# Three loads of one seam moved from SyncE's queue to ScalarE's, in a hybrid mixer block on one Trainium2 core

## The chip, the cores and the metric

The kernel runs on 1 core of one Trainium2 chip. The metric is the device time of one execution in microseconds (us), the median over runs. A core has five engines with queues of their own: TensorE (PE, matmuls; PEld is its weight load), VectorE (DVE), ScalarE (ACT), GpSimd (POOL) and SyncE (SP). In this kernel SP issues nearly all transfers, ACT issues some stores, and each queue runs its instructions strictly in order: what stands behind a waiting instruction waits too.

## The reference

One encoder layer in float32, with 512 frames of width 2048: an input projection, two recurrent mixers (a gated delta rule and RWKV-7), an output projection, cross-attention into 256 memory tokens, and a squared-ReLU MLP.

```python
y = rmsnorm(x) @ W_in
h = x + concat[gdn(y_gdn), rwkv7(y_rwkv)] @ W_out
mn = rmsnorm(mem)                      # 256 memory tokens
k = mn @ wk;  v = mn @ wv              # keys and values
h = h + softmax((rmsnorm(h) @ wq) k^T / sqrt(512)) v @ wo      # 4 heads
h = h + relu(rmsnorm(h) @ w_up)**2 @ w_down
out = rmsnorm(h)
```

## The kernel before, in words

Every float32 weight is split into a rounded part `whi` and a rest `wlo`, and the activations likewise (`xhi`, `xlo`), so a product of near float32 precision takes three fast matmuls. For each weight tile of 128x1024 (512 KB) SP loads `wraw`, ACT casts it to `whi`, DVE subtracts to get `wlo`, and PE multiplies. Three buffers of each kind take turns (`NWR`, `NWS` = 3): the load of tile i+3 can only go out when DVE has finished with tile i.

The first phase, about 0 to 1126 us of the span, is laid out by a planner in the kernel itself. Its functions are generators, called chains, which yield single instructions: `loader` (the weight tiles), `projections` (the matmuls), `rwkv` and `gdn` (the mixers), `presums` and others. `run` keeps a clock per engine, estimates with `cost` when each chain's next instruction could start, and writes the one that could start first, with a chain's rank as a handicap. What comes out is a fixed order per engine. Since every choice follows from the estimates, one different choice early on can shift the whole order behind it. A transfer enters the estimates in `issue`: it costs its queue's clock 330 ns on SP and 60 ns on ACT, and it is taken to land 2.9 us after its issue or later, if earlier transfers fill the bandwidth.

The list `wq` holds the sources of all tiles in their order. Tiles 0 to 117 are the input projection (59 groups `py`, 2 tiles each), with four passes of the memory tokens between them for their squares. Then comes the seam that this document is about, entries 122 to 127: three quarters of the memory tokens (`in_memT`), the first key weight tile (`in_wk`), the last quarter of the memory tokens, the second key weight tile. 30 more key tiles follow and then 32 of the query weights (`in_wqT`). The function `rawload(i)` takes a buffer and yields the load of entry i; `loader` calls it for entry i+3 when it is done with entry i. The function `memory` turns a quarter of the memory tokens into four tiles `mhl` (ACT scales, DVE takes the rest). PE goes from the last `py` over to `kp` (keys, 16 groups of two weight tiles) and then to `kq` (the query weights times the keys). Each `kp` half needs `whi` and `wlo` of one key tile and 8 of the 16 `mhl`.

Between these matmuls the mixers' work is woven in. Here it is: the norm of a GDN key (`gn` on PE, `sg` on ACT, then `gkn`, `gk` on DVE, then `pkk` on PE); and the triangular inverse of the last RWKV pair, whose small blocks POOL solves in `sr`, whose results go out by SP as `bg16T` and `bg16U`, come back as `r` and `E`, and are multiplied together by PE in `ri7x`, `ri7w`, `ri7s`, `ri7t` and `ri7u`, with `k` and `r` updated by DVE in between. The later `gi7` and `gs` are the same for the last GDN head.

`presums` works ahead for the MLP: it loads four blocks of `w_down` in pieces of 410 columns (`ds`), adds and subtracts them on DVE and stores the sums in DRAM. It runs at the lowest priority until the keys are done; what is left over is done in pieces of up to 512 columns (`sl`, `acc`) in the MLP's second half, between 2369 and 2652 us.

Of the kernel before, what the change touches and what calls it, by code (L numbers as in the profile page):

```python
# [73 lines left out]
def build(tc, I, out):  # L74
    nc = tc.nc
# [64 lines left out]
    def wraw():  # L140
        wcnt[0] += 1
        return tile_of(pw, [P, 1024], F32, "wraw", f"wraw{wcnt[0]}", NWR)
# [32 lines left out]
    def tile_of(pool, shape, dt, tag, nm, bufs):  # L175
        t = pool.tile(shape, dt, tag=tag, name=nm, bufs=bufs)
        turns[tag] = turns.get(tag, -1) + 1
        slot[t.tensor.name] = (tag, turns[tag] % bufs)
        holder[tag, turns[tag] % bufs] = t.tensor.name
        return t  # L180
# [27 lines left out]
    DV, AC, GS, TE, SY = (Lane(e, k) for e, k in ((V, "DVE"), (S, "ACT"), (GP, "POOL"), (PE, "PE"), (nc.sync, "SP")))  # L208
# [169 lines left out]
    wq = [("w", I["w_in"][n][:, h * 1024:(h + 1) * 1024]) for h in range(2) for n in range(2)]  # L378
# [36 lines left out]
    wq += [("m", m) for m in mem4[:3]] + hk[:1] + [("m", mem4[3])] + hk[1:]  # L415
    wq += [("w", I["wqT"][n][:, g * 1024:(g + 1) * 1024]) for n in range(KD) for g in range(2)]
    NKP, NKQ = 2 * NIN, 2 * NIN + 2 * KD
    raws, halves, used, whole, piece = {}, {}, set(), set(), {}

    def pieceload(i):  # L420
        piece[i] = tl("sg", 512, NSH["sg"])
        return SY.dma_start(piece[i], wq[i][1][:, 0:512])

    def rawload(i):
        raws[i] = wraw()
        if i in piece:
            return SY.dma_start(raws[i][:, 512:], wq[i][1][:, 512:])
        o = raws[i] if len(wq[i][1].shape) == 2 else raws[i].rearrange("p (a b) -> p a b", b=M)
        return SY.dma_start(o, wq[i][1])

    def loader():
        w = nm = 0
        for i, (kind, _) in enumerate(wq):
            yield lambda: i in raws
            if kind == "w":
                if w in (2, 3):
                    hi, lo = (tile_of(pm, [P, 1024], F32R, t, f"w{t}", 1) for t in ("BK", "AR", "GA", "GB")[2 * w - 4:2 * w - 2])
                else:
                    prev = (w if w < 2 else w - 2) - NWS
                    if prev >= 0:  # L440
                        yield lambda: prev + 2 * (prev > 1) in used
                    hi, lo = halves[w] if w in piece else wsplit()
                if w in piece:
                    yield after("piece", w)
                    yield from split_(raws[i][:, 512:], hi[:, 512:], lo[:, 512:])
                else:
                    yield from split_(raws[i], hi, lo)
                    halves[w] = hi, lo
                whole.add(w)
                w += 1  # L450
            else:
                yield from (memory if kind == "m" else squares)(nm % 4, raws[i])
                nm += 1
            if NWR < i + NWR <= 2 * NWR:
                chain(late(i + NWR), 2)
            elif i + NWR < len(wq):
                yield rawload(i + NWR)
# [7 lines left out]
    def late(i):  # L465
        yield lambda: len(xr) == KD and i - 1 in raws
        yield rawload(i)
# [793 lines left out]
    issue(pieceload(1))  # L1261
    issue(xload(1))
    issue(rawload(0))
    issue(rawload(1))
    for k in range(2, 6):
# [1153 lines left out]
```

## Time and profile before

| | before |
|---|---|
| median of 3 runs | 2902.2 us (2902.17 to 2905.29) |
| profiled execution, its own time | 2904.46 us |
| its span (first to last instruction) | 2902.7 us |
| PE busy | 2870.4 us (99%) |
| DVE, ACT, POOL busy | 2330.4, 1570.0, 223.6 us |
| mean granted TensorE clock | 0.998 |
| seam (last `py`, first `kp`) | about 900 to 938 us of the span |

The span is what the profile covers; 1.8 us of the execution's own time lie outside it. A row of the trace's timeline gives start and length in us, the engine, the line (L256 is the planner's `issue`-time helper, so nearly every planned instruction carries it), the operation, what it writes and reads, and in brackets the idle time ahead of it with what ended that. SPq and ACTq are the transfers' issues on the two queues; their length is the issue, not the transfer. A view of windows gives for each stretch its length, the busy time of PE, PEld, DVE, ACT and POOL with their instruction counts, the granted clock of TensorE (1.00 is full speed), the busy share of the DMA engines and GB/s.

### The profile page before, as it was taken

What the parts mean: (1) busy time and instruction counts of PE and PEld (TensorE: products, weight loads), DVE (VectorE), ACT (ScalarE), POOL (GpSimd) and SP (SyncE); (2) the same over time, 40 slices, a digit from 0 to 9 for tenths busy, and PEclk for the clock granted to TensorE, in tenths of its full rate; (3) what the DMA queues carried; (4) which work ended last, traced back from release to release, by engine and by line L of the source; (5) the groups of instructions that cost most, each with busy time, mean ns of one, the idle gap of its engine ahead of it and who ended that gap; (6) DMA issues with size and microseconds to landing.
All of it is one profiled execution on the core that took longest, in us unless ns stands there. A gap on an engine that the chain in (4) does not pass through costs nothing.

```text
span 2902.7 us, 49242 instructions
## 1 busy us (share of the span) xinstructions
PE 2870.4 (99%) x18794; PEld 2420.3 (83%) x18794; DVE 2330.4 (80%) x3547; ACT 1570.0 (54%) x2233; POOL 223.6 (8%) x547
## 2 busy tenths in 40 slices
PE   8999999999999999999999999999999999999998
PEld 7877877787877888889988888888888888888887
DVE  7787787787887877769956898898998878787888
ACT  6454555555655655564445656555555645454544
POOL 0213213213223000000000000000000000000000
PEclk9999999999999999999999999999999999999999
DMA  5646656656666788784423354565566868978733
GB/s 190 175 139 184 164 156 181 160 150 187 176 163 188 219 249 280 227 286 159 127 92 95 106 163 152 193 199 193 186 201 191 283 225 278 295 257 272 270 100 109
DMA packets 319773, 553.02 MB, mean 191 GB/s; under 512 B 100968, under 2 KB 186220, under 8 KB 319536
## 3 DMA queue, kind: packets, MB, share of 16 engines
q1 hardware_dynamic: 292144, 518.41, 58.0%
q10 hardware_dynamic: 27392, 31.46, 3.1%
q8 instruction: 147, 2.41, 0.3%
q14 instruction: 90, 0.74, 0.1%
HBM read 443.45 MB, written 106.31 MB: 189 GB/s over the span
## 4 chain that ended last, share of the span: by engine, by line
PE 93%; DMA 3%; DVE 2%; ACT 1%; issue 1%; POOL 0%; ACTq 0%; SPq 0%; DVEq 0%; POOLq 0%
PE py L256 22%; PE mxu L256 12%; PE mgu L256 6%; PE mgd L256 6%; PE mxd L256 6%; PE op L122 6%; PE vp L122 3%; PE sc L122 3%; PE at L122 3%; PE mmd L256 3%; PE kp L256 3%; PE mmu L256 3%; PE scrd L256 3%; PE scgd L256 3%; PE kq L256 3%; PE vo L122 1%
## 5 line engine op out<-in xcount | busy, mean ns | idle before, releaser
L256 ACT CAST whi<-wraw 128x1024 fp32r<-128x1024 f32 (+1 forms) x366 | 383.7, 1049 | 399.8 <-PE py L256 146.8
L256 DVE TENSOR_TENSOR wlo<-wraw,whi 128x1024 fp32r<-128x1024 f32 (+1 forms) x366 | 450.4, 1231 | 102.7 <-ACT whi L256 92.9
L256 PE MATMUL py<-xhi,whi 128*128 128x512 f32 x928 | 372.2, 401 | 7.8 <-ACT xhi L256 7.8
L256 PE MATMUL py<-xlo,whi 128*128 128x512 f32 x928 | 373.7, 403 | 0.0
L256 PE MATMUL py<-xhi,wlo 128*128 128x512 f32 x928 | 372.9, 402 | 0.0
L256 ACT CAST whi<-w 128x1024 fp32r<-128x1024 f32 x176 | 185.4, 1054 | 203.9 <-PE mxu L256 48.3
L256 DVE TENSOR_TENSOR wlo<-w,whi 128x1024 fp32r<-128x1024 f32 x176 | 214.8, 1221 | 51.5 <-ACT whi L256 49.5
L256 PE MATMUL mxu<-cb,whi 128*128 128x512 f32 x1016 | 255.0, 392 | 0.0
L256 PEld LDWEIGHTS py<-xhi,whi 128*128 128x128 f32 x928 | 175.0, 189 | 42.1 <-ACT xhi L256 7.8
L256 PEld LDWEIGHTS mxu<-cb,whi 128*128 128x128 f32 x1016 | 182.8, 189 | 32.7
L256 PEld LDWEIGHTS py<-xlo,whi 128*128 128x128 f32 x928 | 175.0, 189 | 35.5 <-DVE xlo L256 0.9
L256 PEld LDWEIGHTS py<-xhi,wlo 128*128 128x128 f32 x928 | 175.1, 189 | 35.1 <-issue 1.8
L131 DVE TENSOR_TENSOR wlo<-wraw,whi 128x1024 fp32r<-128x1024 f32 x112 | 136.6, 1221 | 45.5 <-ACT whi L130 42.5
L130 ACT CAST whi<-wraw 128x1024 fp32r<-128x1024 f32 x112 | 117.7, 1051 | 85.5 <-PE op L122 29.1
L256 PEld LDWEIGHTS mxu<-cb,wlo 128*128 128x128 f32 x1016 | 138.7, 190 | 10.5 <-DVE wlo L256 0.7
L256 PE MATMUL mxu<-cb,wlo 128*128 128x256 f32 x1016 | 142.2, 282 | 0.3 <-DVE wlo L256 0.3
L256 ACT ACT_TABLE_LOAD x87 | 111.6, 1283 | 36.4 <-DVE suml_gn L256 15.5
L256 PE MATMUL mgu<-cb,whi 128*128 128x512 f32 x512 | 129.4, 394 | 1.4 <-ACT whi L256 1.3
L256 PE MATMUL mxd<-whi,cb 128*128 128x512 f32 x512 | 126.7, 389 | 0.0
L256 PE MATMUL mgd<-whi,cb 128*128 128x512 f32 x512 | 126.5, 389 | 0.0
L256 ACT CAST whi<-ws 128x1024 fp32r<-128x1024 f32 x75 | 78.9, 1052 | 75.4 <-PE mgu L256 49.2
L122 PE MATMUL op<-ob,whi 128*128 128x256 f32 (+1 forms) x752 | 115.3, 304 | 0.0
(946 smaller groups left out, 6452.3 us busy)
## 6 DMA issues: line engine op xcount, KB each, us to landing
wraw<-in_w_in SPq DMA_DIRECT2D x116, 512.0 KB, 4.5
wraw<-in_w_up SPq DMA_DIRECT2D x65, 512.0 KB, 3.8
w<-in_w_up SPq DMA_DIRECT2D x63, 512.0 KB, 3.9
ds<-in_w_dm SPq DMA_DIRECT2D x128, 205.0 KB, 4.0
sd_s<-ds SPq DMA_DIRECT2D x128, 205.0 KB, 5.2
wraw<-sd_s SPq DMA_DIRECT2D x51, 512.0 KB, 5.1
w<-sd_s SPq DMA_DIRECT2D x50, 512.0 KB, 5.0
w<-in_w_dm SPq DMA_DIRECT2D x48, 512.0 KB, 5.1
```

Source lines behind the costliest of these rows:

```text
L122: PE.matmul(o, l, r, start=start, stop=stop, skip_group_check=again)
L130: S.copy(hi, src)
L131: V.tensor_tensor(out=lo, in0=src, in1=hi.bitcast(F32), op=ALU.subtract)
L256: f(*a, **k)
```

## The change

Entries 125, 126 and 127 of `wq` (the first key tile, the last quarter of the memory tokens, the second key tile) are issued by ACT instead of SP. `QM` is the entry of the first memory quarter of the seam, 122. Nothing else is edited, and the three transfers are the same as before.

```diff
+    SY_ = SY
     raws, halves, used, whole, piece = {}, {}, set(), set(), {}
 
     def pieceload(i):
         piece[i] = tl("sg", 512, NSH["sg"])
         return SY.dma_start(piece[i], wq[i][1][:, 0:512])
 
+    QM = next(i for i, q in enumerate(wq) if q[0] == "m")
+
     def rawload(i):
         raws[i] = wraw()
+        SY = Lane(nc.scalar, "ACT") if i - QM in (3,4,5,) else SY_
         if i in piece:
             return SY.dma_start(raws[i][:, 512:], wq[i][1][:, 512:])
```

Since the planner prices the three loads differently, it lays out anew what follows, up to about the sixth step of `kq`. From there to the MLP the order on PE, DVE, ACT and SP is as before. Of the summing ahead, 39 pieces of 410 columns instead of 40 are done in the first phase, and the MLP's second half has one piece of `sl` and `acc` more.

On ACT, at the seam (`sg` is the norm of the GDN key, `mhl` the memory tokens), a piece of the difference:

```order
 L256 ACTIVATE sg_10407<-gk_10186 128x512
+L256 DMA wraw_10409<-in_wk 128x1024
+L256 ACTIVATE mhl_10418<-wraw_10149,prm 128x256
+L256 ACTIVATE mhl_10424<-wraw_10149,prm 128x256
+L256 ACTIVATE mhl_10430<-wraw_10149,prm 128x256
+L256 ACTIVATE mhl_10435<-wraw_10149,prm 128x256
 L256 CAST sumh_gn_0_10411_10412<-sg_10407 128x512
```

The first key tile's load stands right behind the first quarter of `mhl` and the square `sg`; the second quarter of `mhl` now precedes the cast for the norm.

Further on in the same queue, of the changed kernel alone (`wraw_10440` is the last memory quarter, `whi_10490` the first key tile's cast):

```order
L256 DMA wraw_10473<-in_wk 128x1024
L256 CAST whi_10490<-wraw_10409 128x1024
L256 ACT_TABLE_LOAD
L256 ACTIVATE sg_10407<-sg_10407 128x512
L256 COPY rstd<-y_184 128x256
L256 ACTIVATE mhl_10519<-wraw_10440,prm 128x256
```

Before, both halves of the norm (`sg`) and their table loads stood ahead of the third quarter of `mhl`, and the key tile's cast came after all of that.

On SP, in the same place, a piece of the difference (`bg16U`, `r`, `E` are the RWKV inverse on its way through DRAM, `sd` the sums' stores):

```order
 L256 DMA bg16U<-sr_10130 64x16x16
-L256 DMA wraw_10409<-in_wk 128x1024
 L256 DMA r_10390<-bg16T 64x8x64 x2
 L256 DMA E_565_10391<-bg16U 64x4x64 x4
-L256 DMA wraw_10446<-in_memT 128x1024
 L256 DMA sd_1_s_154<-ds_55_829 128x410
-L256 DMA wraw_10498<-in_wk 128x1024
```

The three loads leave the places behind the inverse's transfers; the third key tile's load is the first one left on SP, behind three stores of sums.

On DVE, where the RWKV inverse's `k` is made for PE, first before and then in the change:

```order
L256 SCALAR_TENSOR_TENSOR mhl_10528<-wraw_10446,prm,mhl_10528 128x256
L256 TENSOR_TENSOR gEs_10331<-pkk_10504,gEs_10331 128x512
L256 TENSOR_TENSOR wlo_10541<-wraw_10498,whi_10540 128x1024
L256 TENSOR_TENSOR k_10468<-ri7x_10469,cst 128x256
L256 TENSOR_TENSOR k_10468<-ri7w_10470,cst 128x256
L256 TENSOR_TENSOR wlo_10581<-wraw_10508,whi_10580 128x1024
```

```order
L256 SCALAR_TENSOR_TENSOR mhl_10542<-wraw_10440,prm,mhl_10542 128x256
L256 TENSOR_TENSOR wlo_10548<-wraw_10473,whi_10547 128x1024
L256 TENSOR_TENSOR wlo_10575<-wraw_10505,whi_10574 128x1024
L256 TENSOR_TENSOR k_10479<-ri7x_10480,cst 128x256
L256 TENSOR_TENSOR k_10479<-ri7w_10481,cst 128x256
L256 TENSOR_TENSOR gEs_10331<-pkk_10530,gEs_10331 128x512
```

The first `k` stood behind the rest of the second key tile; now it stands behind the rest of the third one too (`wlo_10575`).

On PE, where the last GDN head goes from its inverse (`gi7u`) to its recurrence (`gs`), of the change alone:

```order
L256 MATMUL kp_11748<-mhl_10542,wlo_11713 128x256
L256 MATMUL gi7u_11723<-TtG,gkn_11687 64x64 x4
L256 MATMUL gs_7_0_11832<-gv_11489,TtG 128x128
L256 MATMUL kq_0_0_11834<-khl_10666,whi_11750 128x512
L256 MATMUL kq_0_0_11834<-khl_10717,whi_11750 128x512
```

Before, ten `kp` matmuls stood between `gi7u` and the first `gs`, which reads the `TtG` that DVE makes of `gi7u`; now none does.

## The prediction

> **What bounds the kernel now.** I read the page's head and its chain first, then the windows by stage, the waits of PE, and last the timelines of all queues at the seam.
>
> ```profile
> PE 2870.4 (99%) x18794; PEld 2420.3 (83%) x18794; DVE 2330.4 (80%) x3547; ACT 1570.0 (54%) x2233; POOL 223.6 (8%) x547
> PE 93%; DMA 3%; DVE 2%; ACT 1%; issue 1%; POOL 0%; ACTq 0%; SPq 0%; DVEq 0%; POOLq 0%
> ...
> 900.00:920.00 20.00, 16.58 (x108) 13.41 (x106) 11.37 (x23) 13.01 (x24) 7.79 (x21) 1.00 0.74 189
> 920.00:940.00 20.00, 16.74 (x272) 13.68 (x273) 14.09 (x24) 9.48 (x16) 7.69 (x19) 0.91 0.60 178
> 960.00:980.00 20.00, 20.00 (x180) 17.90 (x179) 18.61 (x36) 9.85 (x16) 0.00 (x0) 1.00 0.63 180
> ...
> PE kp L256 <- ACT whi L256: 2.4, 1, 2.4
> PE pkk L256 <- DVE gk L256: 2.2, 1, 2.2
> PE ri7u L256 <- DVE k L256: 2.0, 1, 2.0
> ```
>
> PE sets the time: it is busy 99% and makes up 93% of the chain. A change can only gain where PE idles or runs slowly, and of 32.3 us of idle time in the whole span (2902.7 less 2870.4) 6.7 lie in the two windows of the seam. The three wait rows are those gaps: 2.2 + 2.4 + 2.0 = 6.6 us. A second loss shows in the clock column, which falls below 1.00 in the second window; in slices of 2 us:
>
> ```profile
> 930.00:932.00 2.00, 0.04 (x1) 0.00 (x0) 1.59 (x3) 1.70 (x3) 1.02 (x2) 1.00 0.26 99
> 932.00:934.00 2.00, 1.97 (x65) 1.71 (x66) 1.97 (x5) 0.21 (x2) 1.61 (x6) 0.84 0.58 145
> 934.00:936.00 2.00, 2.00 (x6) 1.56 (x5) 2.00 (x4) 1.20 (x4) 1.76 (x4) 0.50 0.40 135
> 936.00:938.00 2.00, 2.00 (x12) 1.71 (x11) 0.63 (x1) 0.84 (x1) 1.69 (x5) 0.80 0.75 240
> ```
>
> Behind the third gap the clock is 0.84, 0.50 and 0.80 for 2 us each: 2 x (0.16 + 0.50 + 0.20) = 1.7 us of full-speed work lost. What the seam could give at most is 6.6 + 1.7 = 8.3 us, 0.29% of the time.
>
> Now the cause of the gaps, from the timelines and the chain of waits:
>
> ```profile
> 903.81 0.29 POOL sr L256
> 906.87 0.63 POOL sr L256
> ...
> 906.84 0.58 SPq L256 DMA_DIRECT2D bg16T<-sr  x1
> 908.23 4.19 DMA wraw<-in_wk
> 914.51 5.56 DMA wraw<-in_wk
> 922.46 6.77 DMA wraw<-in_wk
> ...
> 901.47 1.78 DVE L256 SCALAR_TENSOR_TENSOR mhl<-wraw,prm,mhl 128x256 fp32r<-128x256 f32 x4 [0.31 <-ACT mhl L256]
> 911.84 0.69 DVE L256 TENSOR_TENSOR y<-py,rstd 128x512 f32<-128x512 f32 x1 [0.95 <-PE py L256]
> 918.25 1.71 ACT L256 ACTIVATE mhl<-wraw,prm 128x256 fp32r<-128x256 f32 x4 [4.33 <-DMA wraw<-in_memT]
> 920.10 1.04 ACT L256 CAST whi<-wraw 128x1024 fp32r<-128x1024 f32 x1
> 929.33 1.05 ACT L256 CAST whi<-wraw 128x1024 fp32r<-128x1024 f32 x1 [3.60 <-DMA wraw<-in_wk]
> ```
>
> The first key tile's buffer is free when DVE is done with the first memory quarter, at 901.47 + 1.78 = 903.25. SP issues its load only at 908.23, because `bg16T` stands ahead of it and waits until about 906.8 for POOL's solve. The last memory quarter and the second key tile queue up behind that. ACT stands 4.33 us at 918.25 for the memory quarter; the second key tile is cast only at 920.10, and PE's second gap ends there. The third gap has the same root, a tile that landed late, and `k` behind its rest on DVE.
>
> **The change, step by step.** I walk the new orders with the old durations, to see what remains of each gap.
>
> ```profile
> 902.54 0.62 ACT L256 ACTIVATE sg<-gk 128x512 f32<-128x512 f32 x1
> 905.44 1.28 ACT L256 ACT_TABLE_LOAD   x1
> 906.73 0.69 ACT L256 ACTIVATE sg<-gn,cb_e 128x512 f32<-128x512 f32 x1
> 913.95 1.23 DVE L256 TENSOR_TENSOR wlo<-wraw,whi 128x1024 fp32r<-128x1024 f32 x1
> 913.98 1.16 PE L256 MATMUL pkk<-gk,gkn 128*128 128x128 f32 x8 [2.18 <-DVE gk L256]
> 921.20 1.87 PE L256 MATMUL kp<-mhl,whi 128*128 128x512 f32 x7 [2.44 <-ACT whi L256]
> 932.03 0.33 PE L256 MATMUL ri7u<-E,k 64*64 64x64 f32 x4 [1.98 <-DVE k L256]
> 933.46 3.63 PE L256 MATMUL kp<-mhl,whi 128*128 128x512 f32 x8
> ...
> ud<-sl ACTq DMA_DIRECT2D x48, 256.0 KB, 3.9
> xd<-ab ACTq DMA_DIRECT2D x8, 512.0 KB, 3.7
> L256 ACTq DMA_DIRECT2D ud<-sl x48: 364/367/422, 1664.5 to 2282.5; - x48
> ```
>
> *ACT.* Three issues at 0.37 us (the ACTq row) are 1.1 us more on ACT. The first load goes out at 903.3, since `sg` ends at 903.2 and DVE is done at 903.25; ACT hardly waits. The second memory quarter (1.7) and the norm's cast (0.6) take ACT to 905.9; DVE is done with that quarter at about 906.1, so the memory load goes out at 906.2. The third quarter follows until 908.2, a table load until 909.5, the norm's logarithm until 910.1; the second key load goes out at 910.1 to 910.5. The first key tile's cast is 910.5 to 911.5, the second table load and exponential end at 913.4, a copy at 913.7, the last memory quarter at 915.4. How long a load lands on ACT's queue at this place no row shows. The trace bounds it by the key loads on SP, 4.2 and 6.8 us; the stores of ACT's queue lie lower (3.7, 3.9). I take the middle row, 5.6, because it stands in the same crowded stretch. At any of them the first load and the memory quarter are there before ACT comes to them (903.6 + 6.8 = 910.4; 906.5 + 6.8 = 913.3).
>
> *First gap.* PE ends `py` at about 911.8, the cast is done at 911.5, so `kp` starts at once. `pkk` has been moved behind it: the exponential ends at 913.4, then `gkn` and `gk` on DVE (of the size of `y`, 0.69 each) give about 915.0, while PE is through with the first tile at 914.7. Remaining: 0.3 of 2.2.
>
> *Second gap.* The second key tile lands at 910.5 + 5.6 = 916.1, its cast is done at 917.1; PE needs it after `pkk`, at about 916.0. Remaining: 1.1 of 2.4 (0 with a landing of 4.2, 2.3 with 6.8).
>
> *A new wait.* `ri7s` needs `k`, which DVE now does behind the rest of the third key tile. That load stays on SP and goes out when the first tile's rest is done, at 911.84 + 0.69 + 1.23 = 913.8; it lands at 919.4, its cast ends at 920.4, its rest at 921.7, and `k` at 922.4. PE has run out of other work at about 920.3. New: 2.1 us (0.7 to 3.4 with the two bounds).
>
> *Third gap.* The second `ri7u` needs a `k` behind the rest of the sixth key tile. Tile six goes out when tile three's buffer is free (921.7), lands at 927.3, is cast and split by 929.8, and with `khl` and the two `k` steps it is 931.5 to 932.4. PE gets there, with the 15.0 us of work that lies between in the trace (911.8 to the `kp` row at 933.46, less 6.6), one and a half key tiles of 3 us more, and the waits so far, at about 933. Remaining: 0 of 2.0.
>
> Sum at the seam: 6.6 - (0.3 + 1.1 + 2.1) = 3.1 us gained, between 0.9 and 5.6 with the bounds of the landing. The slow clock: it fell after three gaps of at least 2.0 us within 20 us. With one such gap left I take it to stay at 1.00, a gain of 1.7, and keep 0 as the other end.
>
> The Trainium skill's page "TensorE: Matmul & The Clock Gate", Part 1: The HAM clock gate, has the clock halved after an idle window of about 3.4 us and given back after a busy one; the windows run freely. The trace agrees on the half clock and on some 4 us until it is back, but no idle stretch here is longer than 2.44 us, so the condition as the page puts it isn't met and the measurement decides. By its window an estimate of one fall is 3.4 x 0.5 = 1.7 us, the same size.
>
> *Behind the seam.* PE is then earlier by 4.8 us and fully busy, so the lead carries to the end unless something is late. One place is, the last GDN head:
>
> ```profile
> 1025.09 0.38 PE L256 MATMUL gs<-gv,TtG 128*128 128x128 f32 x2
> 1025.51 0.29 DVE L256 COPY gE<-gs 128x128 f32<-128x128 f32 x1 [1.34 <-PE gs L256]
> 1025.90 0.44 PE L256 MATMUL gs<-gE,gkt 128*128 128x128 f32 x2
> 1032.32 0.64 PE L256 MATMUL kq<-khl,whi 128*128 128x512 f32 x2
> ...
> 2620.00:2660.00 40.00, 40.00 (x178) 33.10 (x177) 27.62 (x31) 15.03 (x16) 0.00 (x0) 1.00 0.92 310
> 2660.00:2700.00 40.00, 40.00 (x178) 33.14 (x177) 33.24 (x41) 22.45 (x28) 0.00 (x0) 1.00 0.66 219
> ```
>
> From one `gs` through DVE's copy to the next takes 0.8 us. With no matmul between `gi7u` and the first `gs`, PE waits that trip: 0.8 lost (0 to 2, if a weight tile's rest of 1.2 comes in between on DVE). The next steps have three `kp`-sized matmuls between them, which about cover it.
>
> *The summing ahead.* One piece less in the keys takes four subtractions of 410 columns off DVE. One more piece in the MLP is 8 transfers of 256 KB, 2.1 MB or 6.8 us at 310 GB/s. It comes after 2652 us, beside the window at 2660 with a DMA share of 0.66, and PE made its 178 matmuls per 40 us unslowed even beside the pieces at 0.92. I cost it at nothing; without that cover it is up to 6.8.
>
> Sum: -3.1 - 1.7 + 0.8 = -4.0 us. The profiled execution took 2904.5 us (span 2902.7 and 1.8 around it), which would become 2900.5. The median of the runs, 2902.2, is 2.3 lower, so I forecast 2902.2 - 4.0 = 2898.2 us.
>
> **The rivals.**
> *All three waits go.* If the loads land in 4.2 us, the third key tile too, and the order absorbs the rest, the whole 8.3 less 0.8 comes off: 2902.2 - 7.5 = 2894.7. For it: DMA share is 0.74 at the seam, and the loads now start earlier. Against: `k` stands behind the third tile.
> *The loads move, the time doesn't.* DVE is at 18.61 of 20 us around 970. If PE arrives earlier and DVE can't, PE waits there and the lead is given back: 2902. For it: that row. Against: DVE idled in the seam (11.37 of 20 at 900), so it can also start earlier. The Trainium skill's page "DMA: Bandwidth & Descriptors", section Issuing engines are not separate DMA queues, says that transfers from SP and ACT share the same 16 DMA engines and that a second issuing engine saves only issue time; by that rule this rival is right. The row at 908.23, 5 us behind a free buffer, speaks against it here: what the load loses is not bandwidth but its place behind a waiting instruction.
> *Slower.* The new order between 920 and 1031 has more places like the first `k`, where a step of an inverse or recurrence stands on DVE behind the rest of a tile still on its way. Each costs what the third gap did, 2.0. From two such places on the gain is gone; five of them and one more fall of the clock make -4.0 + 10.0 + 1.7 = +7.7, 2909.9. For it: the third gap was just that, in an order made by the same estimates (2.9 us for a landing that took 4.2 to 6.8). Against: in the window at 960, of the same stage, PE idled nowhere (20.00 of 20).
>
> **How the numbers follow.** Chances: forecast 0.46, all waits gone 0.20, no change 0.16, slower 0.18. About 0.2% (5.8 us, from 2896.4 to 2908.0) is what a measurement of this kernel can tell from no change. Of the forecast a third lies below 2896.4, of the second case nine tenths: faster 0.34. Of the slower case two thirds are past 2908.0: slower 0.12. Within: 0.54. Range: from 2894, all waits gone, to 2906.5, short of the slower case's end; the forecast's own is 2895.5 to 2901.5.
>
> **What would show it.** In the changed profile the first key load is an ACTq row near 903.5 and PE's first `kp` follows `py` with no gap; ACT's 4.33 us for the memory quarter is gone; `ri7s` waits about 2 us for `k` near 921; the clock is 1.00 from 930 to 940; the first `kq` starts about 4 us before 1032.3, and that lead stays in every later stage. I am wrong if a wait of PE for `k`, `gs` or `whi` between 930 and 1040 adds up to more than 4 us, or the lead shrinks between 2650 and 2740.

## The result, and the profile after

The changed kernel takes 2910.9 us (median of 7 runs, 2909.5 to 2912.8); the kernel before, on the same chip, 2902.2 us. The ratio is 1.0033 with a 95% interval of 1.0024 to 1.0042. It is 8.7 us slower, past the bound of 0.2%. I had forecast 2898.2 us, with 12% for slower: the sign was wrong.

From the page of the changed kernel, its windows of 20 us and its list of PE's waits (columns as before: busy time of PE, PEld, DVE, ACT and POOL, then the granted clock):

```profile
PE 2873.7 (99%) x18794; PEld 2423.1 (83%) x18794; DVE 2333.6 (80%) x3547; ACT 1570.9 (54%) x2233; POOL 223.5 (8%) x547
...
900.00:920.00 20.00, 15.90 (x63) 12.83 (x62) 13.69 (x24) 13.59 (x25) 7.67 (x20) 0.85 0.73 185
920.00:940.00 20.00, 18.48 (x277) 15.37 (x279) 14.66 (x25) 9.55 (x15) 3.18 (x8) 0.97 0.75 209
...
PE kp L256 <- ACT whi L256: 7.4, 2, 4.1
PE gs L256 <- DVE TtG L256: 2.0, 1, 2.0
PE ri7s L256 <- DVE k L256: 1.5, 1, 1.5
```

PE still sets the time. Two of the three gaps of before are gone as waits (`pkk` for `gk`, `ri7u` for `k`); the wait of `kp` for `whi` has grown from 2.4 to 7.4 us in two pieces, and `gs` for `TtG` and `ri7s` for `k` are new. The first piece, 4.1 us, lies in the seam. The second, 3.3 us, and the 2.0 us of `gs` lie behind 980, where PE of the kernel before idled 0.3 us. Three stages of PE, first of before, then of the changed kernel, show the whole (busy time, clock, DMA share, GB/s):

```profile
905.00:985.00 80.00, 73.31 (x680) 0.98 0.67 193
985.00:1030.00 45.00, 44.70 (x337) 1.00 0.78 243
1030.00:1080.00 50.00, 50.00 (x298) 1.00 0.81 247
```

```profile
905.00:985.00 80.00, 74.38 (x685) 0.96 0.66 187
985.00:1030.00 45.00, 41.72 (x295) 0.96 0.68 214
1030.00:1080.00 50.00, 48.00 (x290) 0.97 0.68 205
```

What PE loses in a stage is its idle time plus its busy time times what the clock lacks to 1.00. In the seam (905 to 985) that is 6.7 + 1.5 = 8.2 us before and 5.6 + 3.0 = 8.6 after: nothing gained. Behind it, before lost 0.3 us; after loses 3.3 + 1.7 from 985 to 1030 and 2.0 + 1.4 from 1030 to 1080, 8.4 in all. (The clock column has two digits, so each clock term is good to 0.4 us.) The difference of 8.5 us comes near the 8.7 us of the medians, but that closeness is in part chance: the two profiled executions differ by only 5.9 us in span (2908.6 and 2902.7), and outside these stages the one of before idles 1.3 us more. From the end of the last `py` to the end of `kq` the changed kernel takes 7.7 us longer (221.7 against 214.0). So the stages show where the time goes, and its sum to some 3 us. In this account moving the loads costs nothing on balance where they were moved, and the time goes where the planner laid the order anew.

**In the seam**, the timelines of ACT, SP and PE of the changed kernel, and its clock in a slice of 2 us:

```profile
903.37 0.39 ACTq L256 DMA_DIRECT2D wraw<-in_wk  x1
906.13 0.34 ACTq L256 DMA_DIRECT2D wraw<-in_memT  x1
909.59 0.69 ACT L256 ACTIVATE sg<-gn,cb_e 128x512 f32<-128x512 f32 x1
914.12 0.35 ACTq L256 DMA_DIRECT2D wraw<-in_wk  x1
914.51 1.04 ACT L256 CAST whi<-wraw 128x1024 fp32r<-128x1024 f32 x1 [4.23 <-DMA r<-bg16T]
...
906.20 0.58 SPq L256 DMA_DIRECT2D bg16T<-sr  x1
911.18 1.27 SPq L256 DMA_DIRECT2D r<-bg16T  x2
...
915.61 3.78 PE L256 MATMUL kp<-mhl,whi 128*128 128x512 f32 x8 [4.10 <-ACT whi L256]
...
916.00:918.00 2.00, 2.00 (x6) 0.50 0.98 225
```

The first key tile and the memory quarter go out where I put them, at 903.4 and 906.1. The second key tile does not: ACT is free at 910.3 and issues it at 914.1. The releaser named is a transfer of the other queue, the first `r<-bg16T`, issued at 911.18. The first key tile has landed by then (the packets of both earlier loads on ACT's queue are over by 910), but it is cast behind that issue; PE stands for it 4.1 us and then runs at half clock. `bg16T` itself is late: from its issue to that of `r`, which waits for its landing, it is 4.98 us, where before it was 2.53 (906.84 to 909.37).

**Behind 980** two things wait, in the timelines of SP, ACT and PE, and of DVE and PE:

```profile
985.53 1.41 SPq L256 DMA_DIRECT2D sd_s<-ds  x3
991.06 1.28 SPq L256 DMA_DIRECT2D ds<-in_w_dm  x3
992.44 0.38 SPq L256 DMA_DIRECT2D wraw<-in_wk  x1
998.63 1.04 ACT L256 CAST whi<-wraw 128x1024 fp32r<-128x1024 f32 x1 [5.53 <-DMA wraw<-in_wk]
999.73 3.59 PE L256 MATMUL kp<-mhl,whi 128*128 128x512 f32 x8 [3.28 <-ACT whi L256]
...
1033.52 0.68 PE L256 MATMUL gi7u<-TtG,gkn 64*64 64x64 f32 x8
1033.79 1.23 DVE L256 TENSOR_TENSOR wlo<-wraw,whi 128x1024 fp32r<-128x1024 f32 x1 [0.40 <-ACT whi L256]
1034.93 0.42 DVE L256 TENSOR_TENSOR y<-kp,rstd 128x256 f32<-128x256 f32 x1
...
1035.72 0.41 DVE L256 COPY TtG<-gi7u 64x256 f32<-64x256 f32 x1
1036.19 0.49 PE L256 MATMUL gs<-gv,TtG 128*128 128x128 f32 x2 [2.00 <-DVE TtG L256]
```

At 985.5 SP issues three stores of sums; the loads behind them refill the buffers that those stores read, so SP stands until the first store has landed, at 991.06, 5.5 us after its issue. The planner lands a store 2.9 us after its issue, and so put a key tile behind those loads. It goes out at 992.4, lands 6.1 us later, and PE waits 3.3 us. Near 1034 the copy to `TtG` stands on DVE behind the rest of a weight tile and two steps of `y`.

### The profile page after: what moved, and what is told of

It reads as the page before. It is cut to its first block, busy times and chain, and to the rows that moved or that the text cites. A ratio compares the mean times of both kernels' runs of the same rounds, so it can differ in the third digit from the quotient of the medians.

```text
span 2908.6 us, 49252 instructions
## 1 busy us (share of the span) xinstructions
PE 2873.7 (99%) x18794; PEld 2423.1 (83%) x18794; DVE 2333.6 (80%) x3547; ACT 1570.9 (54%) x2233; POOL 223.5 (8%) x547
## 4 chain that ended last, share of the span: by engine, by line
PE 92%; DMA 3%; DVE 2%; ACT 2%; issue 1%; POOL 0%; SPq 0%; ACTq 0%; POOLq 0%; DVEq 0%
PE py L256 21%; PE mxu L256 12%; PE mgu L256 6%; PE mxd L256 6%; PE mgd L256 6%; PE op L122 5%; PE vp L122 3%; PE mmu L256 3%; PE sc L122 3%; PE at L122 3%; PE scrd L256 3%; PE scgd L256 3%; PE mmd L256 3%; PE kq L256 3%; PE kp L256 2%; PE vo L122 2%
```

## The experiments

Each run is compared with runs of the kernel before on its own chip; medians of two chips are not compared. In several kernels single instructions are issued later than planned, with the planner's clocks untouched, by these lines in `issue` (numbers count the calls of `issue`):

```diff
+        LOG[0] += 1
+        n = LOG[0]
+        if n in HOLD:
+            held.setdefault(HOLD[n], []).append((f, a, k))
+        else:
+            f(*a, **k)
+            for f_, a_, k_ in held.pop(n, []):
+                f_(*a_, **k_)
-        f(*a, **k)
```

### What holds ACT: a completion semaphore

In the built program every transfer signals one of eight completion semaphores, given out in turn, and its issue waits for the transfer that had the semaphore last. Both rows of the changed program name number 5, with seven transfers between them:

```
L256 DMA r_564_10390<-bg16T_195 64x8x64 [waits DMAHW5_49,DMAHW3_49]
L256 DMA wraw128_10473<-in_wk 128x1024 [waits DMAHW5_49,DVE_49]
```

In the kernel before, the same two transfers share a semaphore on SP's queue, and there the wait is over in time: `r` had landed at 913.3, and the tile was issued at 914.51. On a second queue the wait ties ACT to what SP has not yet issued. Theory A: this is what holds ACT. Theory B: the queue or the DMA engines do. One small store more ahead of the memory quarter shifts the turn by one, so that the second key tile follows that store; the same store ahead of the first key tile (`== 3`) leaves it behind `r`:

```diff
+        op = SY.dma_start(o, wq[i][1])
+        if i - QM == 4:
+            def first(*a, **k):
+                nc.scalar.dma_start(pd.tile([P, 64], F32, name="xtra", tag="xtra"), cst0[:, 0:64])
+                nc.scalar.dma_start(*a, **k)
+            op = op[:2] + (first,) + op[3:]
+        return op
-        return SY.dma_start(o, wq[i][1])
```

> The changed kernel with one small store (128 x 64, from a constant) issued by ScalarE directly ahead of the load of the last memory quarter; order and plan are otherwise kept. Theory A (completion semaphores): the eight completion semaphores are given to the transfers in turn, and a transfer is not issued before the one that had its semaphore last has landed. The second key tile then follows the small store in its semaphore and no longer the first r<-bg16T. It is issued by ScalarE at about 911 instead of 914.1, the cast behind it starts at about 911.1 instead of 914.5, the gap of 4.1 us ahead of the first kp matmuls falls under 1 us, the fall of the clock behind it goes, and the time is about 2905 us (2903 to 2907.5). Theory B (the queue or the DMA engines hold ScalarE's issue while SP's scattered transfers run): the issue stays at about 914 and the time at 2911.

> The same small store, but issued directly ahead of the first key tile, so that the turn of the semaphores gives the second key tile the one of the first r<-bg16T again. Theory A: no relief, the second key tile is issued at 914 to 914.5, the gap ahead of kp stays at about 4 us, time 2911 (2909 to 2913). Theory B: also 2911. If this kernel is as fast as the one with the store ahead of the memory quarter, the semaphore is not the cause.

ACT and SP, of the first and then of the second kernel:

```profile
913.04 0.34 ACTq L256 DMA_DIRECT2D wraw<-in_wk  x1
914.39 1.04 ACT L256 CAST whi<-wraw 128x1024 fp32r<-128x1024 f32 x1
...
912.51 1.27 SPq L256 DMA_DIRECT2D r<-bg16T  x2
918.80 1.57 SPq L256 DMA_DIRECT2D sd_s<-ds  x3
920.46 9.31 SPq L256 DMA_DIRECT2D wraw<-in_wk  x4
...
906.45 0.91 ACT L256 ACTIVATE mhl<-wraw,prm 128x256 fp32r<-128x256 f32 x2 [2.32 <-DMA ds<-in_w_dm]
929.81 0.48 PE L256 MATMUL ri7s<-k,E 64*64 64x64 f32 x4 [4.93 <-DVE k L256]
```

```profile
916.59 0.36 ACTq L256 DMA_DIRECT2D wraw<-in_wk  x1
916.99 1.05 ACT L256 CAST whi<-wraw 128x1024 fp32r<-128x1024 f32 x1 [1.70 <-DMA r<-bg16T]
...
913.73 1.27 SPq L256 DMA_DIRECT2D r<-bg16T  x2
```

With the turn shifted the tile is issued 0.5 us after `r`, before `r` can have landed, and ACT waits for nothing. In the control it is issued 2.9 us after `r`, with `r` as the releaser. So A holds and B falls. But the time does not follow: 2916.0 us against 2904.3, ratio 1.0038 (1.0025 to 1.0051), and 1.0030 (1.0019 to 1.0042) for the control. In the first kernel the gap ahead of `kp` is gone and `ri7s` waits 4.9 us for `k` instead of 1.5. The 6 us I expected from it did not come.

The profile of the first kernel shows where they went. The second key tile now runs beside `r`, and `r` lands 6.2 us after its issue (918.7), where in the changed kernel it took 2.9. The next store on SP has the semaphore of `r`, so SP stands until 918.80 and issues the third key tile at 920.46 instead of 916.86; the `k` behind that tile's rest is late.

The first key tile, too, shares a semaphore with a transfer on SP, a load of `presums` (`ds`). In the changed kernel's own two profiles the tile goes out 0.5 us after ACT is free. In the two kernels above ACT stands for that load: in the first at the tile itself (2.32 us idle), in the control at the small store that now precedes it. In both PE then waits 2.3 us for the norm (`gn`), a wait that the changed kernel's profiles do not have. PE waits there, 0.8 to 2.3 us, in the profile of every later kernel with the new order and loads on ACT. Why the load of `presums` is late in these and not in the changed kernel is not known. The control's gap ahead of the first `kp` is 0.8 us, where I expected 4: PE had already lost 2.3 us at `gn`.

The second key tile back on SP, the other two on ACT (`in (3, 4)`):

> The second key tile goes back to SP's queue, the first key tile and the memory quarter stay on ScalarE's. Behind this place the order is that of the changed kernel. Theory A: the cast of the first key tile is no longer held (about 910.5 instead of 914.5), and the gap of 4.1 us goes; the second key tile is issued on SP behind the E transfers at about 915.2 and its cast starts at about 920, as late as now. Theory C (the new order itself costs something behind 975: the load that is held by a presum store, 3.3 us, the trip through TtG, 2.0 us, and the clock behind each): these stay, so the time is about 2905 us and not below 2903. If A were all, the time would be 2898 to 2901.

1.0034 (1.0021 to 1.0046). The cast of the first tile is not held, the second is cast at 921.9, and `kp` waits there instead, 3.3 us. The losses behind 975 stay, as C said; the time came out higher than C's number, because the seam gained nothing: PE idles 5.8 us in it (905 to 985), where in the changed kernel it idles 5.6.

### The order and the queue, each alone

`Lane(nc.sync, "ACT")` gives the planner ACT's price and issues on SP: the new order, the old queue. `Lane(nc.scalar, "SP")` gives the old order and the new queue. The changed kernel was run again as a measure for the edits that follow.

> The order of the changed kernel on TensorE, VectorE and ScalarE, with all three loads issued from SP's queue again. It prices the new order alone. Theory C: the three gaps of before between 910 and 940 come back (about 6.6 us with the clock 8.3) and the losses behind 975 stay (3.3 + 2.0 us and the clock behind them, some 3 to 5 us), so 2907 to 2910 us. If the new order costs nothing by itself, 2902 us.

> The order of the kernel before on TensorE, VectorE and ScalarE, with the three loads issued from ScalarE's queue, each at the place in ScalarE's order that its old time gives it. With the run of the new order on the old queue this makes the fourth corner of a square. Theory C (the new order alone is the loss): 2899 to 2904 us, at or under the kernel before. Theory G (a load on a second queue that runs beside the scattered 64 KB transfer bg16T makes that one land 5 to 6.4 us after its issue instead of 2.5, and SP's queue stands for it, so that the third key tile is issued 2.5 to 4 us later): r<-bg16T is issued 4.8 us or more behind bg16T here too, and the time is 2 to 7 us over the kernel before.

> The changed kernel itself, as the measure for the three that follow. Both theories: about 8.7 us (7 to 11) over the kernel before.

| order | loads on SP | loads on ACT |
|---|---|---|
| before | 1 | 0.9993 (0.9984 to 1.0002) |
| new | 1.0032 (1.0020 to 1.0045) | 1.0033 (1.0024 to 1.0042); again 1.0027 (1.0017 to 1.0038) |

PE by stage, first of the new order on SP, then of the old order on ACT:

```profile
905.00:985.00 80.00, 74.65 (x688) 0.98 0.69 192
985.00:1030.00 45.00, 40.97 (x291) 0.96 0.68 210
1030.00:1080.00 50.00, 48.00 (x290) 0.97 0.65 196
```

```profile
905.00:985.00 80.00, 76.52 (x703) 0.98 0.70 203
985.00:1030.00 45.00, 45.00 (x342) 1.00 0.78 242
1030.00:1080.00 50.00, 49.77 (x292) 1.00 0.82 254
```

The order decides, not the queue. The new order loses 9 us behind 985 with all loads on SP. The old order, with the same loads on ACT, loses 0.2 us there, and in the seam 3.5 + 1.5 = 5.0 us where before lost 8.2. In this one profile that is about two thirds of the gain I had looked for. It doesn't show as a measured gain: the median is 1.6 us lower and the interval takes in no change.

### Mending the new order in its two places

Near 985, on SP, two key tiles ahead of the refills; near 1033, on PE and DVE, eight products behind `gi7u` and the copy to `TtG` ahead:

```diff
 DMA sd3_1_s4_157<-ds03_56_830 128x410
-DMA ds01_54_828<-in_w_dm 128x410
-DMA ds02_55_829<-in_w_dm 128x410
-DMA ds00_53_827<-in_w_dm 128x410
 DMA wraw149_11369<-in_wk 128x1024
-DMA ds03_56_830<-in_w_dm 128x410
 DMA wraw150_11405<-in_wk 128x1024
+DMA ds01_54_828<-in_w_dm 128x410
+DMA ds02_55_829<-in_w_dm 128x410
+DMA ds00_53_827<-in_w_dm 128x410
+DMA ds03_56_830<-in_w_dm 128x410
...
 TENSOR_TENSOR ds00_53_827<-ds02_55_829,ds00_53_827 128x410
+COPY TtG_194<-gi7u1_11723 64x4x64
 TENSOR_TENSOR wlo_151_11813<-wraw161_11734,whi_151_11812 128x1024
 TENSOR_TENSOR y2_184<-kp15_11748,rstd_120 128x256
 TENSOR_TENSOR y2_184<-y2_184 128x256
-COPY TtG_194<-gi7u1_11723 64x4x64
```

> The changed kernel with one edit in SP's order near 985: the loads of the 24th and 25th key tile stand ahead of the four presum loads that wait for a presum store to land, instead of behind three of them. Everything else keeps its place. Theory C (the loss is made by the new order behind 975): the wait of 3.3 us for the cast whi near 996 goes, or falls under 1 us, with the fall of the clock behind it (1.5), so 4 to 5 us less than the changed kernel: about 4 us over the kernel before. Theory D (the loss is made between 905 and 940, by what the two queues do to each other, and the later waits only take up slack): the time stays within 1.5 us of the changed kernel.

> The changed kernel with one edit near 1033: the last eight wlo products of kp stand behind the gi7u products instead of ahead of them, and the copy of gi7u to TtG stands ahead of the wlo subtraction and the two y steps on VectorE. Theory C: the wait of gs for TtG falls from 2.0 to under 0.7 us and the clock stays up behind it (1.7), so 2.5 to 3.7 us less than the changed kernel: about 5.5 us over the kernel before. Theory D: within 1.5 us of the changed kernel.

> Both edits at once. Theory C: the two losses add, 6.5 to 8.7 us less than the changed kernel, so about the time of the kernel before (0 to 2.5 us over it), though the three loads are still issued by ScalarE. Theory D: within 2 us of the changed kernel.

Waits of PE in the kernel with the first edit, and the row of PE that waits in the kernel with the second:

```profile
PE gs L263 <- DVE TtG L263: 2.0, 1, 2.0
PE kp L263 <- ACT whi L263: 1.1, 2, 0.6
...
1041.87 0.49 PE L263 MATMUL gs<-gE,gkt 128*128 128x128 f32 x2 [2.34 <-DVE gE L263]
```

The first edit takes the wait of 3.3 us away with the fall of the clock behind it. Its ratio is 1.0016 (1.0008 to 1.0025); its runs are on average 3.3 us (1.8 to 4.8, worked out from the runs of both) under the changed kernel on the same chip. So that place is shown to be a cause, for some two fifths of the loss (3.3 of 8.0 us there). The second edit only moved its wait: `gs` no longer waits for `TtG` but 2.3 us for `gE`, one step on, because the weight rest and the `y` steps now stand ahead of that copy. It gave 1.0040 (1.0028 to 1.0053), slower than the changed kernel. Part of that lies in the seam, which the edit doesn't touch (PE waits 1.4 us for the norm there); why it is slower is not settled. Both edits: 1.0019 (1.0010 to 1.0028), as the first alone.

I then put the weight rest and the `y` steps behind the first three copies of the chain, with the edit on SP:

> The changed kernel with the edit near 985 on SP, and near 1033 with the trip through TtG and gE mended: the last eight wlo products of kp behind gi7u, and the copies to TtG, gE and gEG ahead of the wlo subtraction and of the y steps, which are needed 24 matmuls later. Where the edit of the copy to TtG alone only moved the wait (2.3 us for gE), now no wait over 0.7 us is left there and the clock stays up (1.7): 2 to 3.7 us under the kernel with the edit near 985 alone, about 2 to 3 us over the kernel before. If the wait moves again, to gEG or sg, the time is that of the edit near 985 alone.

2907.9 us against 2903.8, 1.0012 (1.0003 to 1.0022). Against the edit on SP alone that is no measurable difference. The wait moved again, to the second `gE`, which stands on DVE behind the weight rest, both `y` steps and a `khl`:

```profile
1036.63 0.49 PE L263 MATMUL gs<-gE,gkt 128*128 128x128 f32 x2 [1.94 <-DVE gE L263]
```

That the trip is worth 3.4 us is therefore an account of the profile and not shown by a run; no edit took the wait away.

### Mending the seam

Theory E: what the second queue costs is ACT standing at an issue. Theory F: the tiles land too late whatever stands on ACT. On ACT, each load behind what it held up; then with the edit on SP, then with that of the trip too (each `mhl` row here is the four of a memory quarter, the second and then the third):

```diff
 ACTIVATE sg<-gk 128x512
-DMA wraw<-in_wk 128x1024
 ACTIVATE mhl<-wraw,prm 128x256
+DMA wraw<-in_wk 128x1024
 CAST sumh_gn<-sg 128x512
-DMA wraw<-in_memT 128x1024
 ACTIVATE mhl<-wraw,prm 128x256
+DMA wraw<-in_memT 128x1024
 ACT_TABLE_LOAD
 ACTIVATE sg<-gn,cb_e 128x512
-DMA wraw<-in_wk 128x1024
 CAST whi<-wraw 128x1024
 ACT_TABLE_LOAD
 ACTIVATE sg<-sg 128x512
+DMA wraw<-in_wk 128x1024
```

> The changed kernel with one edit in ScalarE's order between 903 and 915: each of the three loads is issued behind the work that it held up (the first key tile behind the four mhl of the second memory quarter, the memory quarter behind the four mhl of the third, the second key tile behind the cast of the first and the Exp), so that a wait of the load holds nothing that TensorE needs. Other engines keep their order. Theory E (what the two queues cost is ScalarE standing at an issue that waits for a transfer of SP's queue to land): the gap ahead of the first kp matmuls (4.1 to 4.4 us) falls under 1.5 us, the fall of the clock behind it (2.7) goes, and the time is 4 to 6 us under the changed kernel, about 3 us over the kernel before. Theory F (the tiles land too late whatever stands on ScalarE): the wait appears again further on in this stage (the cast of the second key tile, ri7s for k) and the time stays within 1.5 us of the changed kernel.

> The edit on ScalarE and the one near 985 on SP (the 24th and 25th key tile ahead of the presum loads). Theory E: the gains add, 7 to 10 us under the changed kernel, 1 us over to 2 us under the kernel before. Theory F: about 2.5 us under the changed kernel, as with the edit on SP alone.

> All three edits: the loads behind the work on ScalarE, the key tiles ahead of the presum loads on SP, the trip mended. Theory E with the new order's two losses taken away: 4 to 6 us under the kernel before, 2898 to 2900 us where that has 2903.8. Theory F: 1 to 3 us over the kernel before.

SP, ACT and PE of the first of these three:

```profile
920.05 10.28 SPq L263 DMA_DIRECT2D wraw<-in_wk  x4
927.68 1.04 ACT L263 CAST whi<-wraw 128x1024 fp32r<-128x1024 f32 x1 [8.48 <-DMA wraw<-in_wk]
930.37 0.48 PE L263 MATMUL ri7s<-k,E 64*64 64x64 f32 x4 [7.35 <-DVE k L263]
```

E falls. ACT no longer stands at its issues, and there is no gap ahead of `kp`. But the third key tile, still on SP, goes out at 920.05 and is cast at 927.7, and PE waits 7.35 us for the `k` behind its rest. 1.0043 (1.0030 to 1.0055); with the edit on SP 1.0031 (1.0019 to 1.0043); with all three 1.0027 (1.0018 to 1.0036), where the wait for `k` is still 5.9 us. The stage is bound by the arrival of its tiles: a wait that is taken out returns at the next tile.

Two swaps in the kernel before, all loads on SP, ask the same without the second queue (`gk` behind `gkn` on DVE and a cast ahead on ACT; two `k` ahead of the rest of the fifth tile):

```diff
 TENSOR_TENSOR gkn_567_10460<-gk_554_10186,sg_566_10407 128x512
+TENSOR_TENSOR gk_569_10481<-gkn_567_10460,gqd_553_10176 128x512
 SCALAR_TENSOR_TENSOR mhl8_10474<-wraw125_10223,prm_72,mhl8_10474 128x256
...
-TENSOR_TENSOR gk_569_10481<-gkn_567_10460,gqd_553_10176 128x512
...
-TENSOR_TENSOR wlo_121_10646<-wraw131_10561,whi_121_10645 128x1024
 TENSOR_TENSOR k_573_10652<-ri7x1_10653,cst_75 128x256
 TENSOR_TENSOR k_573_10652<-ri7w1_10654,cst_75 128x256
+TENSOR_TENSOR wlo_121_10646<-wraw131_10561,whi_121_10645 128x1024
```

> The kernel before, all loads on SP's queue, with two swaps on VectorE and ScalarE alone: gk straight behind gkn (ahead of four mhl and the y that waits for the last py), with the cast of the first key tile ahead of the rstd copy, and the two k of the second inverse step ahead of the wlo subtraction of the fifth key tile. If the gaps are made by what stands ahead on VectorE, the gap of 2.2 us ahead of pkk falls to under 1 us and the one of 2.0 us ahead of ri7u with the clock behind it (1.7) goes: 3 to 5 us under the kernel before. If the tiles' landings are what counts, the waits come back at the next kp and the time is within 1.5 us of the kernel before.

```profile
PE kp L263 <- ACT whi L263: 4.9, 2, 4.0
```

Ratio 1.0000 (0.9991 to 1.0009). Both gaps are gone, and `kp` waits 4.9 us for `whi` where it waited 2.4. The landings count here too.

### What the second queue does to the first

A copy that nothing needs, beside the kernel before, all its loads on SP:

```diff
+            def first(*a, **k):
+                nc.scalar.dma_start(pd.tile([P, 1024], F32, name="stray", tag="stray"), I["wk"][0][:, 0:1024])
+                nc.sync.dma_start(*a, **k)
```

> The kernel before, with one 512 KB transfer more, which nothing needs: ScalarE issues a copy of the first key tile from HBM to HBM near 906, where the load of the first key tile stood. All three loads stay on SP's queue and the order is kept. Theory G: r<-bg16T is issued 4.5 to 6.4 us behind bg16T instead of 2.5, and the time is 1 to 4 us over the kernel before. If transfers on two queues do not hold each other up, it is issued 2.5 us behind it, and the time is within 1.5 us of the kernel before (ScalarE's 0.35 us for the issue).

```profile
907.23 0.58 SPq L256 DMA_DIRECT2D bg16T<-sr  x1
911.11 1.27 SPq L256 DMA_DIRECT2D r<-bg16T  x2
```

`r` follows 3.9 us behind `bg16T`, against 2.53 in the kernel before and 2.53 in the new order on SP. In the runs with a key tile or memory quarter on ACT beside it, it is 4.7 to 6.4 us. So a 512 KB transfer on the other queue does hold the scattered one up, a little less than I expected. That it stands on another queue is not shown to matter: in the new order on SP the first `r`, itself scattered, follows a key tile on the same queue by 1.1 us and takes 4.7 us to land, against 2.9 in the changed kernel. The time does not show the stray copy: 1.0003 (0.9995 to 1.0012).

Only the memory quarter on ACT (`in (4,)`), which keeps PE's order:

> Of the three loads only the last memory quarter goes to ScalarE's queue. The order on TensorE stays that of the kernel before, on VectorE and ScalarE four and three rows move. Theory C: since the order is kept, no loss: the wait of ScalarE for this quarter (4.3 us near 914) goes and the time is 0 to 4 us under the kernel before. Theory G: bg16T lands later here too (r issued 4 us or more behind it), and the time is 0 to 4 us over the kernel before.

1.0004 (0.9995 to 1.0012), no change, though `r` follows `bg16T` by 5.8 us. The wait of ACT for this quarter is gone, the gap ahead of `pkk` is 2.2 us as before, and the clock falls earlier and for longer (0.50 from 918 to 923, before from 934 to 936).

### A version at least as good as both

The old order, three loads on ACT, and three swaps at the seam (the first key tile's issue behind four `mhl`; `gk` behind `gkn`; the first cast ahead of the `rstd` copy and of the second issue), and the same without the first swap:

> The old order with the three loads on ScalarE's queue, and three swaps: the first key tile is issued behind the four mhl of the second memory quarter that its wait for a presum load held up (2.3 us), gk stands straight behind gkn on VectorE, and the cast of the first key tile stands ahead of the rstd copy and of the issue of the second. If what is left there (a gap of 3.5 us ahead of pkk and a fall of the clock worth 1.7) is made by what stands ahead on ScalarE and VectorE, both go: 3 to 6 us under the kernel before, 2898 to 2901 where that has 2904.4. If the tiles' landings set the end of this stage, the wait comes back at a kp or at ri7s, and the time is that of the old order on the new queue, 0 to 3 us under the kernel before.

> The same without the move of the first key tile's issue, which again stands ahead of the four mhl. If the 2.3 us that ScalarE stands at that issue are on the path, it is 1 to 3 us slower than the kernel with all three swaps; if the landings set the end, it is the same within 1.5 us.

0.9993 (0.9984 to 1.0001) and 0.9992 (0.9984 to 1.0001): some 2 us under the kernel before, as the old order on ACT's queue without any swap. Taken by their differences to the kernel before, they are about 10 us under the changed kernel. None of the three intervals excludes no change, and the swap of the first issue is worth nothing that can be measured (2903.2 us with it, 2902.7 without). The old order on ACT's queue had one gap left in the seam, 3.5 us ahead of `pkk`. With the three swaps it is gone, and `kp` waits 4.6 us for `whi` instead:

```profile
PE kp L263 <- ACT whi L263: 4.6, 1, 4.6
```

## Why the prediction was wrong, step by step

- *What bounds the kernel.* Right: PE, and all that moved is idle time and clock of PE.
- *The first two issues on ACT* (903.3 and 906.2). Right in the profile: 903.37 and 906.13. It was in part luck, since the first of them also shares a semaphore, and in later kernels with the same order up to there ACT stood at it.
- *"The second key load goes out at 910.1 to 910.5."* Wrong: 914.12 (its landing then took 5.0 us, where I had 5.6). I walked ACT's queue by its buffers and missed the completion semaphore that the load shares with the first `r`, a wait that stands in the built order of the changed kernel. That it was this wait was shown by shifting the turn. With it the first gap became 4.1 us, not 0.3, and the clock fell behind it, where I had it stay up.
- *Second gap 1.1, third 0, new wait of `ri7s` 2.1.* 0, 0 and 1.5. The mechanism of `ri7s` was right. But I took the gaps as separate terms. They are one debt to the landings: in each kernel in which one of them was removed, it came back at the next tile.
- *Seam: 4.8 us gained.* 0.4 lost by the stages. With the old order 3.2 are gained there by the same account, and with the swaps added 0.6 and 2.1, so moving the loads does part of what I said. (The lower end of 0.9 for the gaps leaves out the 0.3 of the first one; with all the terms at their worst it is 0.6.)
- *"PE is then earlier by 4.8 us and fully busy, so the lead carries to the end unless something is late. One place is."* This is the step that made the sign wrong. I read the new order behind the seam on PE and DVE only. On SP a key tile had come to stand behind three refills of sums that wait for a store: 3.3 us and a fall of the clock, not in my sum at all. The square of order and queue shows that the new order loses 8 to 9 us whatever the queue. My own sign of being wrong, more than 4 us of waits for `k`, `gs` or `whi` between 930 and 1040, came true with 3.3 + 2.0.
- *The last GDN head: 0.8 lost (0 to 2).* 2.0, the end of my range, because a rest of 1.23 us and two `y` steps did come in between; and the clock fell behind it, 1.4 more, which I had not priced.
- *One more piece in the MLP at nothing.* The profiles agree: from PE's first `mgd`, a product of the MLP (2315.2 us before, 2321.2 after), to its last matmul it is 578.0 us in both, so the lag of 6.0 us with which the changed kernel comes there stays 6.0. It wasn't run alone.
- *The sum.* Forecast -4.0, by the stages +8.5. Of the 12.5 between them 5.2 lie in the seam (4.8 gained against 0.4 lost) and 7.3 behind it (0.8 against 8.1).
- *The rivals.* "Slower" had 2909.9 us, near the result by luck, since it came to it by five steps of inverse or recurrence behind late tiles. There was one (`gs`); the other place was a load. "The loads move, the time doesn't" is what the change of queue alone gave, and I gave that rival 0.16. The Trainium skill's page "DMA: Bandwidth & Descriptors", section Issuing engines are not separate DMA queues, says that transfers run on the same 16 DMA engines and interleave whichever engine started them, and that a second issuing engine saves only issue time. The stray copy, which made `bg16T` land 1.4 us later, agrees with it, and so does the ratio of 0.9993.

What stays open: why the kernel with the trip edit alone is slower than the changed one, what the trip is worth by itself, and why the first key tile's issue is held in some kernels with the new order and not in others. Of the 8 us, 3.3 are shown by a run to come from one place; for the rest the runs show that the new order brings it, and the profiles where.

## What to carry to other kernels

When an edit changes the price that a planner sees, the new order is the change: walk every queue of it to the end of the re-laid part, the DMA queue first, and look for a load that stands behind a refill which waits for a store. To learn what the edit itself is worth, run its four corners, order and queue each old and new. Before an issue is moved to another engine's queue, look up which earlier transfer its completion semaphore makes it wait for, and what stands behind it on that engine.

## What the runs showed of the hardware

The issue of a transfer waits for the transfer that had its completion semaphore last, also when that one is on another engine's queue: a key tile on ACT, free to go at 910.3, went out at 914.12, 0.1 us after the `r` on SP had landed, and with the turn shifted it went out while `r` was still on its way.

A small scattered transfer lands much later beside a large one: `bg16T` took 2.5 to 2.7 us with all loads on SP, 3.9 beside one stray 512 KB copy, 4.7 to 6.4 beside the moved loads. `r` took 2.9 us in the changed kernel, and 6.2 with a key tile issued 0.5 us behind it on the other queue.

A gap of the same length at the same place lowered PE's clock in one kernel and not in another. Slices of 2 us behind the wait of `gs` for `gE`, first in the kernel with the edits on SP and on the trip (gap of 1.94 us), then in that with all three edits (1.94 us too):

```profile
1038.00:1040.00 2.00, 2.00 (x6) 0.50 0.62 93
```

```profile
1038.00:1040.00 2.00, 2.00 (x12) 1.00 0.53 207
```

The length of a gap of about 2 us alone does not tell whether 1.5 to 1.7 us of half clock follow. In a forecast such a term needs both ends.
